# In-place masks without the row's constant in the forgetting heads' bias, and negated weights written by GpSimd

## The chip, the cores and the metric

The kernel runs on one core of one Trainium2 chip. The metric is device time in microseconds (us) of one execution. Before the change, three runs took 1092.12 us in the median (1089.89 to 1092.16). The engines are called as in the profile: PE is TensorE, DVE is VectorE, ACT is ScalarE, POOL is GpSimd; SP is SyncE, whose queue issues most of the DMAs.

## The reference

One decoder layer over 512 tokens of width 1024: a half-step SwiGLU FFN, then a mixer of two attention branches with gates, then a second half-step FFN. The change lies in the mixer. Its branch A is a forgetting attention with 8 heads of 64:

```python
def fox_attention(q, k, v, log_f):
    cum = jnp.cumsum(log_f, axis=1).transpose(0, 2, 1)
    ...
        logits = jnp.einsum('bqhd,bkhd->bhqk', q[:, start:end], k[:, :end]).astype(jnp.float32) * scale
        logits = logits + cum[:, :, start:end, None] - cum[:, :, None, :end]
        ...
        logits = jnp.where(kpos <= qpos, logits, NEG_INF)
        p = jax.nn.softmax(logits, axis=-1).astype(v.dtype)
        outs.append(jnp.einsum('bhqk,bkhd->bqhd', p, v[:, :end]))
```

For one query t, `cum[t]` is the same in all of its logits, and a softmax does not change when one number is added to a whole row. Branch B has 8 heads of sparse attention with a top-k indexer. The combined input projection `h @ w_in` feeds both.

## The kernel before

All matrix products take fp32 operands split in two parts, a rounded high part and the rest (wh and wl of a weight, xh and xl of the data). A product is three matmuls: wh by xh, wl by xh, wh by xl (`mm3`, whose three lines are inlined at L133 to L135 in the profile). PE's order is written out by hand; the other engines' orders (ACT, DVE, POOL, SP) come from a scheduler that goes by its own estimates of durations. Each engine and each queue works its instructions off in order, so an instruction that waits holds back all that stand behind it.

The stages in order: FFN 1 (to some 362 us), the mixer's projections and attention, the mixer's output, FFN 2 (from some 752 us).

**Weights.** `load_w` (L116) loads a chunk of 128 x 1024 from memory into a raw tile (ra, rb, rc in turn) by SP; ACT casts it to wh (L123). For most weights wl is raw minus wh by DVE or POOL (L128). For 16 chunks, those of the projections w_fk, w_fq, w_fv and w_dq (`by_dma`, set in `tm256`, L755), wl comes in two steps: ACT writes -wh (L125), and then a DMA issued by POOL reads the chunk from memory once more and adds it in flight (L126). The list `added` keeps these DMAs. A chunk is asked for two chunks before its products run (`weight`, L687); wh and wl have three buffers each.

**Heads.** `prod` runs projections in small steps of matmuls between the steps of the heads, so that PE has work while a softmax is under way. The loop over g (L1045) runs 16 heads, counted from 0: 0 to 7 are the forgetting heads, 8 to 15 the sparse ones. A head has four query blocks of 128 queries, done from the last (512 keys) to the first (128 keys): i = 3, 2, 1, 0, or by columns 512, 384, 256, 128. For each block, `softmax_block` (L907):

- takes the block's bias b from `bias(i)`,
- lets PE compute ps_qk (the logits' negative, L651 and L652),
- lets DVE write p = ps_qk + b and the row's least value mn in one instruction (L914); ACT then computes exp(mn - p) and the row's sum rs (L916), DVE its reciprocal (L917), POOL the product (L918, "normalisation").

The values of a head follow later, in `value_step`: PE transposes p (pt, L925), ACT and DVE split it (ph, L929; pl, L930), PE multiplies with the values (po, L935 and L936), and `head_out` copies the two halves of po (o, o3, L942 and L945), adds them (POOL, L946) and splits them (oAh, L949; oAl, L950). Every second head fetches new queries and keys (`get_q`, `get_k`): PE transposes them (ps_q, ps_k, L626), ACT and DVE split them (L645, L646: st, kh, kl). Their inputs kn were normed by `normed` (ACT squares sqh, L614; DVE sums ss, L616 and L617; POOL takes a power rh, L620, and scales kn, L724). In between DVE works off the indexer's top-k (L862, L864).

**The bias of a forgetting head.** `get_bias(g)` loads the head's row of cumulative sums from memory into all 128 partitions: the tile cb, 128 x 512, two buffers (L985). `bias(i)` writes a new tile b: POOL adds the negative of the block's own cumulative sums, `ncum`, one number for each query (L992), and then sets the part above the diagonal, the last 128 columns of the block, to 1e30 (L993). `ncum` is made once by DVE from `cum` (L849). The tiles b come from the pool "t" with six buffers, which other short-lived tiles share. So before the change cb is read by POOL only, and a buffer of cb is free as soon as POOL has made the four biases, which it often does far ahead of the blocks.

Of the kernel before, what the change touches and what calls it, by code (L numbers as in the profile page):

```python
# [11 lines left out]
F32 = mybir.dt.float32  # L12
F32R = mybir.dt.float32r
AF = mybir.ActivationFunctionType
OP = mybir.AluOpType
# [36 lines left out]
def tile_hybrid_layer(ctx: ExitStack, tc: tile.TileContext, a: dict):  # L52
# [14 lines left out]
    def tmp_tile(name):  # L67
        return tmp.tile([P, T], F32, tag="t", name=name)
# [47 lines left out]
    def load_w(src, n, m, raw=None, at=0, by_dma=False):  # L116
        f = n * m
        if raw is None:
            raw = raw_tile(next(raw_tags))
        wh, wl = (wpool.tile([P, W_COLS], F32R, tag=nm, name=nm)[:, at:at + 1024] for nm in ("wh", "wl"))  # L120
        with tc.high_priority(offset=1 if first else 30):
            nc.sync.dma_start(raw[:, :f].rearrange("p (n m) -> p n m", n=n), src)
            S.copy(wh[:, :f], raw[:, :f])  # L123
            if by_dma:
                S.mul(wl[:, :f], wh[:, :f].bitcast(F32), -1.0)  # L125
                added.append(G.dma_start(wl[:, :f].rearrange("p (n m) -> p n m", n=n), src, accum_op=OP.add))  # L126
            else:
                lo_eng[0].tensor_sub(wl[:, :f], raw[:, :f], wh[:, :f].bitcast(F32))  # L128
        return (wh[:, :f].rearrange("p (n m) -> p n m", n=n),
                wl[:, :f].rearrange("p (n m) -> p n m", n=n))  # L130
# [451 lines left out]
    with ExitStack() as merge_ctx, ExitStack() as mix_ctx, ExitStack() as att_ctx:  # L582
# [9 lines left out]
        dkl = at.tile([P, T], F32R, name="dkl")  # L592
        dvv = at.tile([P, NT, P], F32R, name="dvv")
        cum = at.tile([P, NT, H], F32, name="cum")
        ncum = at.tile([P, NT, H], F32, name="ncum")
        dram = att_ctx.enter_context(tc.tile_pool(name="dram", bufs=1, space=bass.MemoryType.DRAM))
        cum_rows = dram.tile([H, T], F32, name="cum_rows")
        wi = at.tile([P, NT, H], F32, name="wi")
# [4 lines left out]
        def mark(ins, late):  # L603

            marks.append((prod.total + late, ins))
# [217 lines left out]
        def forget():  # L823

            z = small.tile([P, NT, H], F32, tag="z", bufs=1, name="z")
            V.tensor_add(z, sg[:, :, 64:72], bf[:, None, :].to_broadcast([P, NT, H]))
            na = small.tile([P, NT, H], F32, tag="na", bufs=1, name="na")
            V.scalar_tensor_tensor(na, z, -1.0, z, op0=OP.mult, op1=OP.min)
            e = small.tile([P, NT, H], F32, tag="e", bufs=1, name="e")
            S.activation(e, na, AF.Exp)  # L830
            u1 = small.tile([P, NT, H], F32, tag="u1", bufs=1, name="u1")
            V.tensor_scalar(u1, e, 1.0, None, op0=OP.add)
            ln = small.tile([P, NT, H], F32, tag="ln", bufs=1, name="ln")
            S.activation(ln, u1, AF.Ln)
            cr = small.tile([P, NT, H], F32, tag="cr", bufs=1, name="cr")
            V.tensor_scalar(cr, u1, 1.0, None, op0=OP.subtract)
            V.tensor_sub(cr, e, cr)
            V.reciprocal(u1, u1)
            V.tensor_mul(cr, cr, u1)
            V.tensor_add(ln, ln, cr)  # L840
            lf = small.tile([P, NT, H], F32, tag="lf", bufs=1, name="lf")
            V.scalar_tensor_tensor(lf, z, 0.0, ln, op0=OP.min, op1=OP.subtract)
            yield
            pc = psum.tile([P, T], F32, tag="s", bufs=2, name="pc")
            for t in range(NT):
                for j in range(t + 1):
                    PE.matmul(pc[:, t * H:(t + 1) * H], trin if j == t else ones, lf[:, j], start=(j == 0), stop=(j == t))
            V.tensor_copy(cum, pc[:, :NT * H].rearrange("p (t h) -> p t h", t=NT))
            mark(V.tensor_scalar(ncum, cum, -1.0, None, op0=OP.mult), 0.5)  # L849
            yield  # L850
            ps = psum.tile([P, T], F32, tag="s", bufs=2, name="ps_ct")
            for t in range(NT):
                PE.transpose(ps[0:H, t * P:(t + 1) * P], cum[:, t], ident)
            cum_t = tmp_tile("cum_t")[0:H]
            S.copy(cum_t, ps[0:H])
            S.dma_start(cum_rows, cum_t)
# [126 lines left out]
        def get_bias(g):  # L983
            cb = at.tile([P, T], F32, tag="cb", bufs=2, name="cb")
            nc.sync.dma_start(cb, cum_rows[g:g + 1, :].to_broadcast([P, T]) if g < H else a["rel"][g - H])  # L985

            def bias(i):
                n = P * (i + 1)
                b = tmp_tile("b")
                if g < H:  # L990
                    with tc.issue_after(added[-2].ins) if g == 0 else nullcontext():
                        G.tensor_scalar(b[:, :n], cb[:, :n], 1.0, ncum[:, i, g:g + 1], op0=OP.mult, op1=OP.add)  # L992
                    G.affine_select(out=b[:, i * P:n], in_=b[:, i * P:n], compare_op=OP.is_ge, fill=BIG, base=0,  # L993
                                    pattern=[[-1, P]], channel_multiplier=1)
                else:
                    G.tensor_sub(b[:, :n], sc[i] if i else cpos, cb[:, T - n:T])
                return b[:, :n]
            return bias

# [192 lines left out]
```

## Time and profile before

| what | value |
|---|---|
| median of three runs | 1092.12 us (1089.89 to 1092.16) |
| the profiled execution | 1090.95 us, its span 1088.9 us |
| PE busy from 362 to 436 us (top-k scores, first projections) | 74.0 of 74 us |
| PE busy from 436 to 546 us (heads 0 to 7) | 101.7 of 110 us |
| PE busy from 660 to 752 us (gates, output) | 92.0 of 92 us |
| TensorE clock granted, mean of the span | 0.998 |

A row of the profile's groups reads: line, engine, operation, tiles written <- read with their shapes, count; then busy us and mean ns of one; then the idle time of the engine just before, and what ended it. A wait list names the waiting instruction, then the one that ended the wait: us in total, how often, the longest.

### The profile page before, as it was taken

The page shows a single profiled execution, that of the slowest core. Times are in us where ns is not written, and L with a number is a line of the kernel's source. Part 1 is how long each engine was busy: PE and PEld are TensorE (multiplying, and loading weights), DVE is VectorE, ACT ScalarE, POOL GpSimd, SP SyncE. Part 2 cuts the span into 40 slices and gives each one's busy share as a digit, 9 for nine tenths or more (in the row PEclk, how much of TensorE's full clock was granted, in tenths as well). Part 3 has the DMA queues.
Part 4 walks back from the last instruction along what each step waited for, and adds up shares of the span by engine and source line. Part 5 has one row for each costly group of instructions (what it writes and reads, how often), then busy time and mean ns, then how long its engine had stood idle before and what let it go on. Part 6 is the DMA issues. An engine that isn't in the chain of part 4 may idle for free.

```text
span 1088.9 us, 17859 instructions
## 1 busy us (share of the span) xinstructions
PE 1070.5 (98%) x6880; PEld 968.1 (89%) x6880; DVE 795.0 (73%) x1287; ACT 575.4 (53%) x908; POOL 209.4 (19%) x280
## 2 busy tenths in 40 slices
PE   9999999999999999999999999999999999999998
PEld 7889899989998899988778778889998899989997
DVE  6896478755967489879764765879986588865974
ACT  5554155522555675877655785455663155522650
POOL 0000000000001316677752740000110001000100
PEclk9999999999999999999999999999999999999999
DMA  7434335523442268765124211425574356633552
GB/s 239 118 98 134 108 88 147 139 95 97 125 108 90 99 134 195 173 143 133 49 59 135 87 60 48 135 89 153 138 166 137 90 135 160 165 97 98 145 126 78
DMA packets 43572, 131.01 MB, mean 120 GB/s; under 512 B 5336, under 2 KB 5720, under 8 KB 43488
## 3 DMA queue, kind: packets, MB, share of 16 engines
q1 hardware_dynamic: 35120, 107.58, 32.5%
q0 software_dynamic: 8208, 22.02, 11.7%
q8 instruction: 54, 0.88, 0.3%
q10 hardware_dynamic: 160, 0.28, 0.1%
q14 instruction: 30, 0.25, 0.1%
HBM read 117.79 MB, written 2.11 MB: 110 GB/s over the span
## 4 chain that ended last, share of the span: by engine, by line
PE 85%; DVE 6%; ACT 4%; issue 2%; DMA 2%; POOL 1%; SPq 0%; DVEq 0%; POOLq 0%; ACTq 0%
PE pd L133 7%; PE pd L135 7%; PE pd L134 7%; PE pB L133 5%; PE pB L134 5%; PE pB L135 5%; PE pC L133 3%; PE pA L133 3%; PE pA L134 3%; PE pC L134 3%; PE pC L135 3%; PE pA L135 3%; PE ps_f L133 3%; PE ps_f L134 3%; PE ps_f L135 3%
## 5 line engine op out<-in xcount | busy, mean ns | idle before, releaser
L133 PE MATMUL pd<-ah,wh 128*128 128x512 f32 (+1 forms) x294 | 113.2, 385 | 0.0
L134 PE MATMUL pd<-al,wh 128*128 128x512 f32 (+1 forms) x294 | 113.1, 385 | 0.0
L135 PE MATMUL pd<-ah,wl 128*128 128x512 f32 (+1 forms) x294 | 113.1, 385 | 0.0
L112 ACT CAST wh<-s 128x1024 fp32r<-128x1024 f32 x57 | 60.1, 1054 | 99.1 <-PE pB L134 51.3
L133 PE MATMUL pB<-tbh,wh 128*128 128x256 f32 x304 | 85.0, 280 | 0.6 <-DVE u L435 0.6
L134 PE MATMUL pB<-tbl,wh 128*128 128x256 f32 x304 | 84.8, 279 | 0.0
L135 PE MATMUL pB<-tbh,wl 128*128 128x256 f32 x304 | 84.7, 279 | 0.0
L133 PE MATMUL ps_t<-wh,xh 128*128 128x256 f32 (+1 forms) x288 | 81.7, 284 | 0.0
L134 PE MATMUL ps_t<-wl,xh 128*128 128x256 f32 (+1 forms) x288 | 81.0, 281 | 0.0
L135 PE MATMUL ps_t<-wh,xl 128*128 128x256 f32 (+1 forms) x288 | 81.0, 281 | 0.0
L271 POOL DMA_DIRECT2D al<-gu x26 | 22.2, 856 | 260.5 <-ACT al L270 248.9
L113 DVE TENSOR_TENSOR wl<-s,wh 128x1024 fp32r<-128x1024 f32 x57 | 69.4, 1218 | 1.7 <-ACT wh L112 1.5
L393 POOL DMA_DIRECT2D s<-in_w_pair_dram x11 | 9.6, 877 | 297.9 <-DVE wl L113 297.9
L135 PEld LDWEIGHTS pd<-ah,wl 128*128 128x128 f32 x294 | 55.2, 188 | 11.1
L134 PEld LDWEIGHTS pd<-al,wh 128*128 128x128 f32 x294 | 55.2, 188 | 10.8
L133 PEld LDWEIGHTS pd<-ah,wh 128*128 128x128 f32 x294 | 55.2, 188 | 10.8
L133 PEld LDWEIGHTS pB<-tbh,wh 128*128 128x128 f32 x304 | 57.1, 188 | 1.1 <-issue 0.9
L134 PEld LDWEIGHTS pB<-tbl,wh 128*128 128x128 f32 x304 | 57.2, 188 | 0.0
L135 PEld LDWEIGHTS pB<-tbh,wl 128*128 128x128 f32 x304 | 57.2, 188 | 0.0
L134 PEld LDWEIGHTS ps_t<-wl,xh 128*128 128x128 f32 x288 | 55.1, 191 | 0.5
L133 PEld LDWEIGHTS ps_t<-wh,xh 128*128 128x128 f32 x288 | 55.0, 191 | 0.5
L135 PEld LDWEIGHTS ps_t<-wh,xl 128*128 128x128 f32 x288 | 55.0, 191 | 0.0
(355 smaller groups left out, 3611.9 us busy)
## 6 DMA issues: line engine op xcount, KB each, us to landing
rc<-in_w_pair_dram SPq DMA_DIRECT2D x16, 512.0 KB, 3.6
rb<-in_w_pair_dram SPq DMA_DIRECT2D x16, 512.0 KB, 3.6
ra<-in_w_pair_dram SPq DMA_DIRECT2D x15, 512.0 KB, 3.6
rd<-in_w_pair_dram SPq DMA_DIRECT2D x15, 512.0 KB, 3.7
re<-in_w_pair_dram SPq DMA_DIRECT2D x14, 512.0 KB, 3.7
al<-gu POOLq DMA_DIRECT2D x26, 256.0 KB, 4.7
s<-in_w_pair_dram POOLq DMA_DIRECT2D x11, 512.0 KB, 5.6
ra<-in_w_down_dram SPq DMA_DIRECT2D x7, 512.0 KB, 3.6
```

Source lines behind the costliest of these rows:

```text
L112: S.copy(wh[:, :f], raw[:, :f])
L113: V.tensor_sub(wl[:, :f], raw[:, :f], wh[:, :f].bitcast(F32))
L133: PE.matmul(out, lh, rh, start=start, stop=False, **more)
L134: PE.matmul(out, lh, rl, start=False, stop=False, **more)
L135: PE.matmul(out, ll, rh, start=False, stop=stop, **more)
L271: G.dma_start(l, u, accum_op=OP.add)
L393: G.dma_start(t["s2"], load["b"][2], accum_op=OP.add)
```

## The change

For heads 0 to 7 the bias is no longer a tile of its own. `bias(i)` sets the 128 columns at the diagonal to 1e30 in cb itself and returns the first columns of cb; the number per query is left out, and with it `ncum` (a tile of the same size keeps its place). Since blocks run from the last to the first, the columns that one selection overwrites are not read by later blocks. But the block before has read them: the selection of block i - 1 writes columns that p of block i reads, so it waits for that p. And cb is now read by DVE, up to the last block of the head, before its buffer takes the row of the head after next. In `load_w` the negation -wh is made by POOL in place of ACT, with one multiplication by -1 and one by 1.

```diff
             if by_dma:
-                S.mul(wl[:, :f], wh[:, :f].bitcast(F32), -1.0)
+                G.tensor_scalar(wl[:, :f], wh[:, :f].bitcast(F32), -1.0, 1.0, op0=OP.mult, op1=OP.mult)
                 added.append(G.dma_start(wl[:, :f].rearrange("p (n m) -> p n m", n=n), src, accum_op=OP.add))
...
-        ncum = at.tile([P, NT, H], F32, name="ncum")
+        at.tile([P, NT, H], F32, name="pad")
...
-            V.tensor_copy(cum, pc[:, :NT * H].rearrange("p (t h) -> p t h", t=NT))
-            mark(V.tensor_scalar(ncum, cum, -1.0, None, op0=OP.mult), 0.5)
+            mark(V.tensor_copy(cum, pc[:, :NT * H].rearrange("p (t h) -> p t h", t=NT)), 0.5)
...
             def bias(i):
                 n = P * (i + 1)
-                b = tmp_tile("b")
                 if g < H:
                     with tc.issue_after(added[-2].ins) if g == 0 else nullcontext():
-                        G.tensor_scalar(b[:, :n], cb[:, :n], 1.0, ncum[:, i, g:g + 1], op0=OP.mult, op1=OP.add)
-                    G.affine_select(out=b[:, i * P:n], in_=b[:, i * P:n], compare_op=OP.is_ge, fill=BIG, base=0,
-                                    pattern=[[-1, P]], channel_multiplier=1)
-                else:
-                    G.tensor_sub(b[:, :n], sc[i] if i else cpos, cb[:, T - n:T])
+                        G.affine_select(out=cb[:, i * P:n], in_=cb[:, i * P:n], compare_op=OP.is_ge, fill=BIG, base=0,
+                                        pattern=[[-1, P]], channel_multiplier=1)
+                    return cb[:, :n]
+                b = tmp_tile("b")
+                G.tensor_sub(b[:, :n], sc[i] if i else cpos, cb[:, T - n:T])
                 return b[:, :n]
             return bias
```

PE's order stays the same. The lines after L849 move up by one, those after L992 by two. The scheduler lays out ACT, DVE, POOL and SP anew. Three places of that order follow; numbers behind a name tell one buffer's use from another's.

First, POOL ahead of the second half of the queries that heads 4 and 5 take (kn). Before, the rows behind head 2's biases:

```order
L126 DMA wl_4984<-in_w_dq_dram 128x1024
L993 AFFINE_SELECT b_5112<-b_5112 128x128
L620 TENSOR_TENSOR rh_4977<-ss_4974,nhalf_100 128x8
L126 DMA wl_5091<-in_w_dq_dram 128x1024
L724 TENSOR_TENSOR kn_4969<-kn_4969,rh_4977 128x512
```

And in the changed kernel, where cb_5120 is the row of head 4, cb_4901 that of head 3, and p_5044 the last block of head 2:

```order
L620 TENSOR_TENSOR rh_4956<-ss_4953,nhalf_100 128x8
L917 TENSOR_SCALAR p_5044<-p_5044,rs_4857 128x128
L125 TENSOR_SCALAR wl_5066<-wh_5065 128x1024
L990 AFFINE_SELECT cb_5120<-cb_5120 128x128
L990 AFFINE_SELECT cb_4901<-cb_4901 128x128
L724 TENSOR_TENSOR kn_4948<-kn_4948,rh_4956 128x512
```

A normalisation, a multiplication and two selections now stand between rh and kn. The first selection waits for the row of head 4, the second for p of head 3's first block.

Second, DVE around head 2's blocks of 256 and 128 columns. Before (head 2 is the one with rs_4874):

```order
L930 TENSOR_TENSOR pl_5010<-pt_5005,ph_5009 128x384
L950 TENSOR_TENSOR oAl_3405<-o_4933,oAh_3401 64x512
L616 TENSOR_REDUCE ss_4974<-sqh_4972 128x8
L930 TENSOR_TENSOR pl_5054<-pt_5050,ph_5053 128x256
L617 TENSOR_SCALAR ss_4974<-ss_4974 128x8
L864 MATCH_REPLACE sc2_3399<-m8_5016,sc2_3399 128x384
L862 MAX m8_5059<-sc3_3400 128x8
L914 ISA p_5026,mn_4873<-ps_qk_5023,b_5018 128x256
L914 ISA mn_4873 128x1
L914 ISA p_5069,mn_4873<-ps_qk_5066,b_5061 128x128
```

And in the changed kernel:

```order
L617 TENSOR_SCALAR ss_4942<-ss_4942 128x8
L913 ISA p_5003,mn_4856<-ps_qk_5000,cb_4685 128x256
L913 ISA mn_4856 128x1
L916 RECIPROCAL rs_4857<-rs_4857 128x1
L929 TENSOR_TENSOR pl_4989<-pt_4984,ph_4988 128x384
L949 TENSOR_TENSOR oAl_3405<-o_4914,oAh_3401 64x512
L616 TENSOR_REDUCE ss_4953<-sqh_4951 128x8
L913 ISA p_5044,mn_4856<-ps_qk_5041,cb_4685 128x128
```

The p of 256 columns moved from behind pl, oAl, ss and another pl to ahead of them, and the p of 128 columns to right behind ss.

Third, DVE around head 6's block of 256 columns. Before:

```order
L617 TENSOR_SCALAR ss_5854<-ss_5854 128x8
L128 TENSOR_TENSOR wl_5898<-ra_5896,wh_5897 128x1024
L930 TENSOR_TENSOR pl_5876<-pt_5871,ph_5875 128x384
L950 TENSOR_TENSOR oAl_3407<-o_5811,oAh_3403 64x512
L616 TENSOR_REDUCE ss_5865<-sqh_5863 128x8
L930 TENSOR_TENSOR pl_5915<-pt_5911,ph_5914 128x256
L617 TENSOR_SCALAR ss_5865<-ss_5865 128x8
L930 TENSOR_TENSOR pl_5944<-pt_5941,ph_5943 128x128
L914 ISA p_5890,mn_5760<-ps_qk_5887,b_5882 128x256
```

And in the changed kernel:

```order
L617 TENSOR_SCALAR ss_5801<-ss_5801 128x8
L913 ISA p_5835,mn_5711<-ps_qk_5832,cb_5553 128x256
L913 ISA mn_5711 128x1
L128 TENSOR_TENSOR wl_5843<-ra_5841,wh_5842 128x1024
L929 TENSOR_TENSOR pl_5823<-pt_5818,ph_5822 128x384
L949 TENSOR_TENSOR oAl_3407<-o_5760,oAh_3403 64x512
```

Here too the p stands ahead of the weight subtraction L128 and of the three pl that were in front of it.

## The prediction

> **What bounds the kernel now.** I read the busy times first, then the same times cut by stage, then what TensorE (PE) waits for in the one stage where it waits, and last the rows around each of those waits.
>
> ```profile
> PE 1070.5 (98%) x6880; PEld 968.1 (89%) x6880; DVE 795.0 (73%) x1287; ACT 575.4 (53%) x908; POOL 209.4 (19%) x280
> ```
>
> PE is busy for all but 18.4 us of the span. A change that touches no matrix product can win or lose only PE's idle time, so the question is where that idle time lies. The view by stretches has, for each stretch, its length and each engine's busy time (instructions):
>
> ```profile
> 362.00:436.00 74.00, 74.00 (x506) 68.97 (x505) 58.83 (x159) 51.76 (x97) 28.41 (x29) 0.98 0.61 150
> 436.00:546.00 110.00, 101.72 (x749) 94.33 (x748) 87.93 (x249) 83.17 (x177) 78.92 (x121) 1.00 0.52 125
> 546.00:660.00 114.00, 110.72 (x565) 90.72 (x564) 70.98 (x173) 75.89 (x156) 52.71 (x70) 1.00 0.26 82
> ```
>
> The changed lines run from 375 us to 546 us. Up to 436 us PE is never idle, so nothing can be won there. From 436 to 546 us, which are heads 0 to 7, it idles 8.3 us while DVE, ACT and POOL are busy for 80%, 76% and 72%. That is the whole stake. The 3.3 us after it lie in heads 8 to 15, and the rest at both ends of the span; their code stays. PE's waits in the stake (us in total, times, longest):
>
> ```profile
> PE pt L925 <- DVE st L646: 2.7, 3, 1.7
> PE ps_qk L651 <- DVE mn L914: 2.2, 2, 1.2
> PE po L936 <- DVE pl L930: 1.1, 2, 0.9
> PE ps_k L626 <- DVE pl L930: 0.8, 1, 0.8
> PE pt L925 <- DVE pl L930: 0.4, 1, 0.4
> PE ps_q L626 <- POOL kn L724: 0.4, 1, 0.4
> PE pt L925 <- POOL p L918: 0.3, 1, 0.3
> PE po L935 <- ACT ph L929: 0.2, 1, 0.2
> PE po L935 <- ACT o L945: 0.2, 1, 0.2
> ```
>
> Most end with DVE, but none with the biases (b) or with a weight. So the biases and the negated weights cost time only through the queue places they hold on POOL and ACT, ahead of what DVE needs. The six large waits one by one (start, duration, and in brackets the idle time before):
>
> ```profile
> 452.80 0.66 PE L626 MATMUL ps_k<-ident,kn 128*128 128x128 f32 x4 [0.81 <-DVE pl L930]
> 454.18 0.55 PE L925 MATMUL pt<-ident,p 128*128 128x128 f32 x3 [0.72 <-DVE st L646]
> 475.61 0.50 PE L651 MATMUL ps_qk<-kh,st 128*128 128x512 f32 x1 [1.25 <-DVE mn L914]
> 511.13 0.55 PE L925 MATMUL pt<-ident,p 128*128 128x128 f32 x3 [1.67 <-DVE st L646]
> 518.20 0.38 PE L936 MATMUL po<-pl,fv 128*128 128x256 f32 x1 [0.94 <-DVE pl L930]
> 530.51 0.50 PE L651 MATMUL ps_qk<-kh,st 128*128 128x512 f32 x1 [0.95 <-DVE mn L914]
> ```
>
> **What the change moves, in engine time.** The groups of instructions that it touches, and those nearest to the new one (busy us, mean ns):
>
> ```profile
> L125 ACT ACTIVATE wl<-wh 128x1024 fp32r<-128x1024 f32 x16 | 16.9, 1056 | 0.2
> L992 POOL TENSOR_SCALAR b<-cb,ncum 128x512 f32<-128x512 f32 (+3 forms) x32 | 19.4, 673 | 0.2
> L993 POOL TENSOR_SCALAR_AFFINE_SELECT b<-b 128x128 f32<-128x128 f32 x32 | 10.4, 378 | 0.3
> L918 POOL TENSOR_SCALAR p<-p,rs 128x512 f32<-128x512 f32 x16 | 11.6, 728 | 22.8 <-DVE rs L917 10.9 <-PE pt L925 10.3 <-PE po L936 1.6
> L918 POOL TENSOR_SCALAR p<-p,rs 128x128 f32<-128x128 f32 x16 | 6.5, 404 | 22.1 <-DVE rs L917 22.0
> L128 POOL TENSOR_TENSOR wl<-rc,wh 128x1024 fp32r<-128x1024 f32 x2 | 4.8, 2393 | 6.1 <-ACT wh L123 6.1
> ```
>
> ACT loses 16 negations, 16.9 us. POOL loses 32 bias additions, 19.4 us, and keeps the 32 selections. It gains 16 multiplications of 1024 columns, which the trace does not show. At least one costs the 0.73 us of half the columns (L918, 512), at most the 2.39 us of the two-input operation of that size (L128). I take the line through the two L918 rows, (728 - 404) / 384 = 0.84 ns a column, so 0.73 + 0.43 = 1.16 us, since L918 is the same operation; 16 make 18.6 us. POOL's total stays within 1 us, and what changes is what stands where. The Trainium skill, GPSIMD Engine Reference, section 3.1, gives 1.03 cycles a column for bodies of up to two operations; at that page's 1.2 GHz this is an estimated 0.88 us each and 14.1 us in all, 4.5 us less than by the rows. No run yet shows which holds for 1024 columns.
>
> **The weights** are costed at nothing. The multiplication starts when ACT's cast is done, as the negation did. The narrowest chunk is this one: its adding DMA on POOL, the landing of such DMAs (KB, us), and PE's first product with the chunk.
>
> ```profile
> 409.40 0.88 POOL L126 DMA_DIRECT2D wl<-in_w_fv_dram  x1 [2.83 <-DVE m L862]
> wl<-in_w_fv_dram POOLq DMA_DIRECT2D x4, 512.0 KB, 5.8
> 417.36 0.28 PE L133 MATMUL ps_t<-wh,xh 128*128 128x256 f32 x1
> ```
>
> Issued at 409.4 it lands at about 415.2 us, and PE begins at 417.4. So 2.2 us hide a later start; beyond that each 1 us late is 1 us of PE.
>
> **The ACT terms.** Rows of ACT around the first and the third wait, and of DVE behind them:
>
> ```profile
> 449.63 1.05 ACT L125 ACTIVATE wl<-wh 128x1024 fp32r<-128x1024 f32 x1
> 450.58 0.67 ACT L645 ACTIVATE st<-ps_q,gq 64x512 fp32r<-64x512 f32 x1
> 470.72 1.06 ACT L125 ACTIVATE wl<-wh 128x1024 fp32r<-128x1024 f32 x1
> 471.68 0.63 ACT L614 ACTIVATE sqh<-kn 128x512 f32<-128x512 f32 x1
> ```
>
> ```profile
> 472.34 0.69 DVE L616 TENSOR_REDUCE ss<-sqh 128x8 f32<-128x512 f32 x1 [0.77 <-ACT sqh L614]
> 475.15 0.40 DVE L914 CUSTOM_DVE_ANT_0 p<-ps_qk,b 128x256 f32<-128x256 f32 x1
> 516.59 1.22 DVE L128 TENSOR_TENSOR wl<-rc,wh 128x1024 fp32r<-128x1024 f32 x1
> ```
>
> At 449.63 the negation stands straight ahead of the query split that DVE sits waiting for. Without it the split and the pl behind it come 0.95 us earlier, and the wait of 0.81 us goes. The second wait grows by about 0.2 us, because another block's p now stands between the two splits on DVE: **-0.6 us** for the pair.
>
> PE had made the product of head 2's 256-column block here:
>
> ```profile
> 468.71 0.28 PE L652 MATMUL ps_qk<-kl,st 128*128 128x256 f32 x1
> ```
>
> Its p starts 6 us later, at 475.15, and PE waits for it at 475.61. In between p waited in DVE's queue behind rows that waited for sqh, itself behind the negation at 470.72. In the new order p stands ahead of pl, oAl and ss (second order excerpt). I take the 1.25 us as gone: **-1.25 us**. At 530.51 it is the same: p of head 6's 256 columns now stands ahead of the weight subtraction and of three pl (third excerpt): **-0.95 us**. At 518.20 the pl stood behind the subtraction of 516.59. The p ahead of it come earlier now, so it starts about 1 us earlier: **-0.9 us**. The two waits for ACT, 0.4 us in all, go with its 16.9 us, **-0.4 us**. The wait at 511.13 is for the second query split, which stays behind p and pl: **0**. Where PE waits 0.4 us for a pl (pt, L930), one more p comes ahead of it: **+0.5 us**. A remainder of 0.1 us elsewhere goes.
>
> **The POOL terms.** Three rows: POOL's scaling of the queries of heads 4 and 5, the landing of the broadcast row (KB, us), and the spread of one small DVE operation:
>
> ```profile
> 477.70 1.62 POOL L724 TENSOR_TENSOR kn<-kn,rh 128x512 f32<-128x512 f32 x1
> cb<-cum_rows SPq DMA_DIRECT2D x8, 256.0 KB, 3.7
> L617 DVE TENSOR_SCALAR ss<-ss x16: 142/160/850, 403.2 to 528.7; 128x8 f32<-128x8 f32 x12, 128x1 f32<-128x1 f32 x4
> ```
>
> The kn of 477.70 is what PE's ps_q wait of 0.4 us ended on. PE arrives there 1.9 us earlier by the terms above, but on POOL a multiplication (1.16 us) and two selections now stand ahead of kn (first excerpt), one of them waiting for a row that lands 3.7 us after the last p of head 2. I put kn's end at 478.5 us, 0.8 us earlier than now. So PE waits about 1.7 us there, and the 1.0 us of small waits around 480 us go: **+0.7 us**. With the multiplication at 0.73 us this becomes +0.3, at 2.39 us +1.9.
>
> The new wait in place: a selection writes what the p before it reads, so it waits for DVE, and p of the next block waits for it. Behind it on POOL wait the normalisations, kn, and the adding DMAs. Between two blocks lie 110 / 32 = 3.4 us, and a selection takes 0.38 us, so DVE does not feel it unless something long stands between. The one such place that I find is the normalisation of head 4's last block, which now stands behind head 6's first selection and its row: **+0.3 us**.
>
> The sum is -0.6 - 1.25 - 0.95 - 0.9 - 0.4 + 0.5 - 0.1 + 0.7 + 0.3 = **-2.7 us**. The profiled execution took 1090.95 us (span 1088.9, and 2.05 around it), so it would become 1088.25. The median of the three runs, 1092.12, lies 1.17 above it; I predict that median less 2.7, **1089.4 us**.
>
> **The rivals.**
>
> The waits only move (within 0.2%, which is 2.2 us and about what a measurement of this kernel can tell from no change). DVE is busy 80% of the stage, and wherever PE comes earlier it meets the next late row, as at kn. If half of the 3.1 us of the two p terms and the pl term come back that way, 1.1 us are left: 1091.0 us. The 87.93 us of DVE work, which the change leaves alone, speak for it.
>
> POOL's order becomes the bound (slower). The row of head g+2 can be loaded only after DVE's last p of head g; before, POOL was done with it early. Its first selection stands on POOL ahead of the second selection of head g+1, whose p comes two blocks, 6.9 us, later. From the issue, 3.7 us of landing and two selections of 0.38 take some 4.5 us. It decides from the point where another 2.4 us are lost between, which two multiplications ahead on POOL would be. If that costs 1 us at each of heads 2 to 7, the sum is +6 - 2.7 = +3.3 us: 1095.4 us. For it speaks POOL's long queue, against it that the slack holds at every place I followed.
>
> POOL's multiplications hold DVE up (slower). L617 takes 160 ns in the middle and 850 ns at worst, so some DVE rows are held by 0.7 us. Eight of the 16 negations lie in the stake; if each of the eight multiplications held a DVE row on the way to PE by 0.7 us, 5.6 - 2.7 = +2.9 us: 1095.0 us. Against it, the 19.4 us of additions that go could hold DVE in the same way. The Trainium skill, SBUF — State Buffer, section on the two separate sides, states that the pair of ports shared by VectorE and GpSimd is an exclusive lock, held for a whole instruction. The spread of L617 agrees with that; by it one long multiplication would hold a row longer than a short addition did.
>
> Everything that was late comes early. If also the wait at 511.13 and the new one at kn fall away, 2.7 + 1.7 + 1.7 = 6.1 us: 1086.0 us.
>
> **How the numbers follow.** The forecast, from 2.2 to 4.5 us faster, gets 0.37 and the larger gain 0.13: faster 0.50. Waits that only move get 0.35: same. POOL's order gets 0.10 and the ports 0.05: slower 0.15. For 8 in 10 I cut the largest gains at 1085.8 us and the slow cases at 1094.6 us, which also holds both ends of the multiplication's price (0.4 us to one side, 1.2 us to the other) and the 2.3 us by which the three runs differ.
>
> **What would show it.** Right: no L125 on ACT, PE's waits from 436 to 546 us at about 5.6 us instead of 8.3, none for mn, one of 1 to 2 us at ps_q for kn. Wrong: waits of PE or DVE ended by the selections, waits of PE for a weight (ps_t), or multiplications far from 1.16 us. If waits before p grow while the ones named here go, POOL's order is the cause.

## The result and the profile after

The changed kernel takes 1100.3 us in the median (four runs, 1097.86 to 1102.53), the kernel before, on the same chip, 1091.0 us (1089.04 to 1092.16). The ratio is 1.0089, 95% interval 1.0074 to 1.0104: 9 us slower, where 2.7 us faster were forecast, and above the range's upper end of 1094.6 us. The profiled execution took 1099.98 us (span 1098.2 us), 9.0 us more than the one before.

First the busy time of the engines on the page of the changed kernel, and then the same three stretches that the prediction shows:

```profile
PE 1073.6 (98%) x6880; PEld 971.1 (88%) x6880; DVE 797.2 (73%) x1286; ACT 561.4 (51%) x892; POOL 209.9 (19%) x264
```

```profile
362.00:436.00 74.00, 72.54 (x505) 67.36 (x504) 59.20 (x155) 43.08 (x87) 34.80 (x33) 1.00 0.62 147
436.00:546.00 110.00, 98.21 (x718) 92.61 (x717) 85.11 (x236) 74.27 (x161) 71.68 (x98) 0.95 0.52 123
546.00:660.00 114.00, 111.08 (x558) 91.40 (x557) 71.06 (x179) 73.21 (x155) 52.30 (x72) 0.99 0.28 84
```

The engines' work came out as expected: 14 us less on ACT, the same on POOL. The loss has three parts. From 436 to 546 us PE idles 11.8 us instead of 8.3, and ahead of that, where it never idled, 1.5 us: 5.0 us. PE's own busy time rises by 3.1 us for the same 6880 matmuls; the clock column, 0.95 instead of 1.00, says why. The third part is 1.0 us at the start of the span, where the code is the same, by the rows of the first 25 us before and after. Over all the traces of this study PE idles from 2.1 to 3.6 us there, so nothing shows that this part is the change's:

```profile
0.00:25.00 25.00, 22.44 (x91) 17.34 (x92) 16.49 (x23) 15.97 (x24) 1.65 (x12) 1.00 0.69 230
```

```profile
0.00:25.00 25.00, 21.41 (x87) 16.23 (x88) 16.48 (x23) 15.90 (x24) 1.66 (x12) 1.00 0.66 220
```

Together 9.1 of the 9.3 us by which the span grew. PE's waits from 436 to 546 us after the change:

```profile
PE po L935 <- DVE pl L929: 3.1, 3, 1.7
PE ps_k L626 <- DVE pl L929: 3.0, 2, 2.7
PE ps_q L626 <- POOL kn L724: 2.8, 1, 2.8
PE pt L924 <- DVE rs L916: 1.7, 2, 1.0
PE pt L924 <- DVE st L646: 0.9, 1, 0.9
PE pt L924 <- DVE pl L929: 0.2, 1, 0.2
```

None ends with mn any more, as forecast, but two of 2.7 and 2.8 us are new, and the longest of po for a pl is 1.7 us in place of 0.9. From the list of all waits from 362 to 560 us, those of POOL for a cast, and those of and for the selections:

```profile
POOL wl L125 <- ACT wh L123: 29.0, 11, 6.5
POOL cb L990 <- DMA cb<-cum_rows: 18.6, 8, 6.0
POOL cb L990 <- DVE mn L913: 6.7, 6, 1.6
DVE p L913 <- POOL cb L990: 6.5, 2, 4.1
```

POOL stands 18.6 us waiting for rows to land, and DVE's p waits twice for POOL. The longer of the two, in order of time, with SP's issue of head 2's row (cb), the selections and the p:

```profile
445.45 0.27 DVE L913 CUSTOM_DVE_ANT_0 p<-ps_qk,cb 128x128 f32<-128x128 f32 x1
...
445.75 0.33 SPq L984 DMA_DIRECT2D cb<-cum_rows  x1
...
447.05 0.69 DVE L913 CUSTOM_DVE_ANT_0 p<-ps_qk,cb 128x512 f32<-128x512 f32 x1 [0.39 <-PE ps_qk L652]
...
453.10 0.54 POOL L990 TENSOR_SCALAR_AFFINE_SELECT cb<-cb 128x128 f32<-128x128 f32 x2 [5.97 <-DMA cb<-cum_rows]
453.67 0.56 DVE L913 CUSTOM_DVE_ANT_0 p<-ps_qk,cb 128x384 f32<-128x384 f32 x1 [4.07 <-POOL cb L990]
...
455.88 1.09 PE L626 MATMUL ps_k<-ident,kn 128*128 128x128 f32 x4 [2.74 <-DVE pl L929]
```

The last p of head 0 at 445.45 frees the buffer, SP issues the row at once, and it lands 7.2 us later. POOL's row at 453.10 holds two selections: head 2's first, which needs that row, and right behind it in the queue head 1's second, which needed nothing but has waited all the same. So the p of head 1's second block starts 6.6 us behind that of the first, the next pl is late, and PE waits 2.74 us for it.

The second time it is head 5's row, issued behind the last p of head 3 and 6.6 us on its way. Its selection stands ahead of that for head 4's second block:

```profile
495.90 0.33 SPq L984 DMA_DIRECT2D cb<-cum_rows  x1
...
502.55 0.54 POOL L990 TENSOR_SCALAR_AFFINE_SELECT cb<-cb 128x128 f32<-128x128 f32 x2 [3.77 <-DMA cb<-cum_rows]
...
503.12 0.56 DVE L913 CUSTOM_DVE_ANT_0 p<-ps_qk,cb 128x384 f32<-128x384 f32 x1 [2.42 <-POOL cb L990]
...
505.33 0.50 PE L935 MATMUL po<-pl,fv 128*128 128x512 f32 x1 [1.69 <-DVE pl L929]
```

### The profile page after: what moved, and what is told of

Its sections match the earlier page's. It is cut to its first block, busy times and chain, and to the rows that moved or that the text cites. A ratio compares the mean times of both kernels' runs of the same rounds, so it can differ in the third digit from the quotient of the medians.

```text
span 1098.2 us, 17837 instructions
## 1 busy us (share of the span) xinstructions
PE 1073.6 (98%) x6880; PEld 971.1 (88%) x6880; DVE 797.2 (73%) x1286; ACT 561.4 (51%) x892; POOL 209.9 (19%) x264
## 4 chain that ended last, share of the span: by engine, by line
PE 84%; DVE 8%; ACT 2%; DMA 2%; issue 2%; POOL 1%; SPq 0%; DVEq 0%; POOLq 0%; ACTq 0%
PE pd L134 7%; PE pd L133 7%; PE pd L135 7%; PE pB L133 5%; PE pB L134 5%; PE pB L135 5%; PE pC L134 3%; PE pC L133 3%; PE pA L134 3%; PE pA L133 3%; PE pC L135 3%; PE pA L135 3%; PE ps_f L133 3%; PE ps_f L134 3%; PE ps_f L135 3%
```

## The experiments

Each time below is a median beside runs of the kernel before on the same chip, with the ratio to these and its 95% interval. The groups ran on different chips, so kernels of different groups are better compared by the ratio.

| kernel | us | ratio | interval |
|---|---|---|---|
| cb3 | 1102.17 | 1.0098 | 1.0077 to 1.0119 |
| mult_only | 1093.92 | 1.0026 | 1.0016 to 1.0035 |
| bias_only | 1090.62 | 1.0004 | 0.9993 to 1.0014 |
| cb3_act | 1090.42 | 1.0000 | 0.9990 to 1.0009 |
| in_turn | 1089.89 | 0.9997 | 0.9987 to 1.0006 |
| one_back | 1094.24 | 1.0044 | 1.0029 to 1.0060 |
| swap_act | 1093.57 | 1.0023 | 1.0013 to 1.0033 |
| in_turn_act | 1087.95 | 0.9972 | 0.9963 to 0.9981 |
| swap_free | 1089.89 | 0.9998 | 0.9988 to 1.0008 |
| in_turn_act3 | 1087.84 | 0.9975 | 0.9966 to 0.9984 |
| in_turn_act_ol | 1089.49 | 0.9990 | 0.9975 to 1.0005 |
| in_turn_cum | 1090.41 | 0.9998 | 0.9989 to 1.0007 |
| in_turn_first8 | 1090.72 | 0.9997 | 0.9987 to 1.0006 |
| in_turn_last8 | 1091.38 | 1.0007 | 0.9998 to 1.0016 |
| last8_stt | 1092.38 | 1.0015 | 1.0006 to 1.0023 |
| in_turn_stt | 1091.14 | 1.0000 | 0.9991 to 1.0009 |
| after_stt | 1099.54 | 1.0077 | 1.0055 to 1.0099 |
| in_turn_act_stt | 1088.81 | 0.9981 | 0.9972 to 0.9989 |

### First: which part of the change

Each part alone, and a third buffer for the rows. **mult_only** is the kernel before with the line of `load_w`; **bias_only** is the changed kernel without it:

```diff
-                S.mul(wl[:, :f], wh[:, :f].bitcast(F32), -1.0)
+                G.tensor_scalar(wl[:, :f], wh[:, :f].bitcast(F32), -1.0, 1.0, op0=OP.mult, op1=OP.mult)
```

> The kernel before with one line of the change alone: GpSimd writes the negated weights; the biases are as before, with ncum and tiles of their own. ROW and INPLACE: 1089 to 1092 us, as before or up to 2 us less, since ACT's negations go. MULT: 1096 to 1101 us, since POOL now works 16.9 us more than in the changed kernel's rivals and the biases of 19.4 us are still there (POOL busy about 227 us).

> The changed kernel with the negation back on ACT: the bias part of the change alone. ROW: the late rows stay, about 1097 to 1100 us. MULT: 1089 to 1092 us. INPLACE: about 1097 to 1100 us.

**cb3** (the changed kernel) and **cb3_act** (bias_only) give every third head a tile that is idle in this stage:

```diff
-            cb = at.tile([P, T], F32, tag="cb", bufs=2, name="cb")
+            cb = tmp.tile([P, T], F32, tag="ssq", bufs=1, name="cb") if g < H and g % 3 == 2 else at.tile([P, T], F32, tag="cb", bufs=2, name="cb")
```

> The changed kernel with a third buffer for the rows cb: heads 2 and 5 take a tile that is idle in this stage, so a row can be loaded one head earlier. ROW (a buffer of cb is held until DVE's last p of the head, so that the row of head g+2 comes late and holds up the selections and all that stands behind them on POOL): the waits of POOL for rows (18.6 us in the changed kernel) fall below 6 us, PE's waits in heads 0 to 7 fall from 13.2 to about 8 us, time about 1092 us, 8 us less than the changed kernel. MULT (GpSimd's multiplications fill POOL's queue ahead of kn and the normalisations): nothing changes, about 1100 us. INPLACE (each selection waits for the p of the block before): nothing changes, about 1100 us.

> The bias part of the change alone (negation on ACT) with the third buffer for cb. ROW: about 1091 us, the waits of POOL for rows gone, PE's waits in heads 0 to 7 at 7 to 9 us. MULT: about 1090 us whether or not the buffer is there, the same as the bias part alone. INPLACE: about 1098 us, the same as the bias part alone, and PE or DVE waits that selections end.

The bias part alone moves the time by nothing that can be told (ratio 1.0004), the multiplications alone cost 2.8 us by the ratio, and both together 9.7 us. So neither part alone is the cause, and INPLACE falls. MULT has the times of bias_only and cb3_act right, but mult_only is 2 us below its range, so it falls as the whole story. ROW has only the time of cb3_act right (1090.42 us), and not by its reason: POOL still waits 15.8 us for rows there, and bias_only takes as long without the buffer. In cb3 the third buffer took nothing away. But it did not do what was meant. With a buffer more, the scheduler moved the first selections one head earlier in POOL's queue, so that they again stand just behind the issue of their rows:

```profile
440.13 0.29 POOL L990 TENSOR_SCALAR_AFFINE_SELECT cb<-cb 128x128 f32<-128x128 f32 x1 [6.27 <-DMA cb<-cum_rows]
```

This is head 2's first selection in cb3: its row is issued at 431.69 us and lands 8.4 us later, and head 0's later selections stand behind it. POOL's waits for rows grew to 24.3 us. The buffer was the wrong knob; the place in the queue had to be held.

What differs between bias_only and the changed kernel at the place shown above is one order. In bias_only head 1's second selection stands ahead of head 2's first one:

```profile
442.78 0.33 SPq L984 DMA_DIRECT2D cb<-cum_rows  x1
...
444.47 0.69 DVE L913 CUSTOM_DVE_ANT_0 p<-ps_qk,cb 128x512 f32<-128x512 f32 x1
...
445.25 0.29 POOL L990 TENSOR_SCALAR_AFFINE_SELECT cb<-cb 128x128 f32<-128x128 f32 x1 [0.38 <-DVE mn L913]
...
448.26 0.56 DVE L913 CUSTOM_DVE_ANT_0 p<-ps_qk,cb 128x384 f32<-128x384 f32 x1 [1.23 <-PE ps_qk L652]
...
449.66 0.29 POOL L990 TENSOR_SCALAR_AFFINE_SELECT cb<-cb 128x128 f32<-128x128 f32 x1 [4.12 <-DMA cb<-cum_rows]
```

The row takes 6.8 us to land here too, and POOL waits 4.1 us for it, but p (448.26) waits for PE alone. In all, POOL waits for rows longer in this kernel (20.1 us) than in the changed one, and it costs nothing.

### Second: the order of the selections

**in_turn** (the changed kernel) and **in_turn_act** (bias_only) hold each head's first selection on POOL behind the last one of the head before:

```diff
-                    with tc.issue_after(added[-2].ins) if g == 0 else nullcontext():
-                        G.affine_select(
+                    with tc.issue_after(added[-2].ins if g == 0 else sel[g - 1, 0].ins) if i == NT - 1 else nullcontext():
+                        sel[g, i] = G.affine_select(
```

> The changed kernel, with each head's first selection held on POOL behind the last selection of the head before it. ORDER (a first selection that waits for a row stands on POOL ahead of the next block's selection, and so the landing of the row, up to 7.2 us, falls on DVE's p): no p waits for a selection by more than 1 us, p of head 1's second block starts within 3.5 us of the first one (6.6 us in the changed kernel), the 2.7 us wait of PE for ps_k goes; what is left is the multiplications' own cost as in the kernel with them alone: about 1094 us. MULT-SUM (the multiplications cost 9 us in any kernel whose selections wait for p, whatever the order of the selections): 1098 to 1101 us.

> The bias part of the change alone (negation on ACT), with each head's first selection held behind the last selection of the head before it: the likely best. ORDER: the few waits of p for selections go: 1088 to 1090.5 us. MULT-SUM: 1090 to 1092 us, no change to the bias part alone.

**one_back** does it at one place, for head 2's first selection (`sel[1, 2]` for g = 2 alone). **swap_act** does the reverse: in bias_only it makes head 2's first selection when its row is asked for, and holds head 1's second selection behind it:

```diff
+            if g == 2:
+                bias(NT - 1)
...
-                    with tc.issue_after(added[-2].ins) if g == 0 else nullcontext():
+                    with tc.issue_after(added[-2].ins if g == 0 else sel[2, 3].ins) if g == 0 or (g, i) == (1, 2) else nullcontext():
```

> The changed kernel with one order alone turned back: head 2's first selection stands on POOL behind head 1's second selection, as it does with the negation on ACT. ORDER: PE's 2.7 and 0.9 us waits at 456 to 458 us and the low clock behind them go: 1094 to 1097 us, 3 to 6 less than the changed kernel's 1100. MULT-SUM: 1099 to 1101 us.

> The bias part of the change alone (negation on ACT), with one order forced: head 2's first selection stands on POOL ahead of head 1's second selection, as the scheduler has it in the changed kernel. ORDER: p of head 1's second block waits for the row of head 2, some 3 to 5 us, and PE 2 to 4 us: 1093 to 1096 us, against 1090.6 without. MULT-SUM: no change, 1090 to 1092 us.

All four went as ORDER expects, and in_turn further: 1089.9 us where 1094 was expected. In in_turn seven selections stand at other places on POOL than in the changed kernel; every other order, on all engines, is the same. One order turned back wins 5 us by the ratio, 6 by the medians; all of them win the whole 10. In one_back PE's 2.7 us wait is gone, but its wait of 0.9 us for st stays, and head 2's row now holds up later blocks: PE waits 2.27 us for a pl at 462.53 us, with the low clock behind it. One order forced costs 2 us by the ratio (1.0023 against 1.0004), 3 by the medians, with the same rows as in the changed kernel, the p at 451.53 waiting 4.0 us and PE 2.66 us:

```profile
450.96 0.54 POOL L992 TENSOR_SCALAR_AFFINE_SELECT cb<-cb 128x128 f32<-128x128 f32 x2 [5.60 <-DMA cb<-cum_rows]
451.53 0.56 DVE L913 CUSTOM_DVE_ANT_0 p<-ps_qk,cb 128x384 f32<-128x384 f32 x1 [4.01 <-POOL cb L992]
...
453.74 0.63 PE L626 MATMUL ps_k<-ident,kn 128*128 128x128 f32 x4 [2.66 <-DVE pl L929]
```

in_turn_act beats both kernels: 1087.95 us, ratio 0.9972. It is the one kernel of these four with neither the harmful order nor the multiplications.

### Third: the row or the place

**swap_free** keeps the forced order of swap_act, but gives head 2's row a tile of its own, so that it is loaded at the start; heads 2 to 4 are held at their places on POOL, and the place of head 1's second selection stays (the first selections of heads 3 and 4 and one kn still moved by a few places):

```diff
+            cb = tmp.tile([P, T], F32, tag="ssq", bufs=1, name="cb") if g == 2 else at.tile([P, T], F32, tag="cb", bufs=2, name="cb")
```

> The kernel with the forced order (negation on ACT, head 2's first selection ahead of head 1's second on POOL), but with a tile of its own for head 2's row, so that the row is loaded at the start and not after DVE's last p of head 0. ROW (what costs is that the selection waits for the row's release and landing): p of head 1's second block starts within 4 us of the first one, PE's 2.7 us wait at 453 us and the low clock behind it go, 1089.5 to 1091.5 us. PLACE (a selection at that place costs by itself, through POOL's time or its wait for a p): 1093 to 1094 us, as with the forced order.

**in_turn_act3** is in_turn_act with the third buffer of cb3; the orders of POOL and DVE are the same as without it.

> Selections in turn, negation on ACT, and a third buffer for the rows; the orders of POOL and DVE are the same as without it. ROW: once the selections are in turn, a row has a whole head to land, so that loading it another head earlier brings nothing: 1087 to 1089 us, the same as with two buffers. If the release of the two buffers still cost something: 1 us less or more.

Both went as ROW expects. With the row there in time, the same order costs nothing: 1089.89 us, and the p of head 1's second block starts 3.8 us behind the first (444.49 to 448.29) instead of 6.6 in swap_act. And with the selections in turn, an earlier row brings nothing (1087.84 against 1087.95). So it takes both, the late row and the place in the queue. A last kernel of this group, **in_turn_act_ol**, moves the subtraction for oAl from DVE to POOL:

```diff
-            (V if gg < H else G).tensor_sub(o2[1][h // 2][own], o[own], o2[0][h // 2][own].bitcast(F32))
+            (V if gg < 0 else G).tensor_sub(o2[1][h // 2][own], o[own], o2[0][h // 2][own].bitcast(F32))
```

> Selections in turn, negation on ACT, and the subtraction that makes oAl (L949) moved from DVE to POOL for heads 0 to 7, into the time that the bias additions left free there. If DVE's queue is what PE waits for now: PE's waits for DVE rows fall by 1 to 2 us, 1085.5 to 1087.5 us. If POOL's queue carries it on (the subtraction stands ahead of normalisations or kn): 1088 to 1091 us.

It is no gain, 1089.49 us: PE's wait for kn grew from 1.2 to 2.1 us, so the subtraction went into POOL's queue ahead of kn.

### Fourth: what the multiplications cost

They cost 2.8 us in mult_only and 1.9 us in in_turn against in_turn_act, with no wait of PE for a weight (ps_t) in any trace. What PE waits for in mult_only, most of all:

```profile
PE ps_qk L651 <- DVE mn L914: 5.7, 4, 1.9
PE pt L925 <- DVE st L646: 1.9, 3, 0.9
PE ps_ct L853 <- DVE cum L848: 1.5, 1, 1.5
```

So with the biases left as they were, PE waits 5.7 us for mn, where it waited 2.2 before. One order on DVE differs with them: the copy of cum stands behind the subtraction dkl, and PE waits 1.5 us for cum at 426 us, in the changed kernel, cb3, mult_only and in_turn. **in_turn_cum** puts dkl behind cum:

```diff
-            evac_split(transposed(lambda t: sd[0][:, t].rearrange("p a d -> p (a d)"), "ps_dk"), hg[:, 3:4], dkh, dkl)
+            ps = transposed(lambda t: sd[0][:, t].rearrange("p a d -> p (a d)"), "ps_dk")
+            S.mul(dkh, ps, hg[:, 3:4])
+            yield
+            with tc.issue_after(copied[0].ins):
+                mark(V.scalar_tensor_tensor(dkl, ps, hg[:, 3:4], dkh.bitcast(F32), op0=OP.mult, op1=OP.subtract), 1.0)
```

> Selections in turn and GpSimd's multiplications, with one order on DVE turned back: the copy of cum stands ahead of the subtraction dkl (0.73 us), as it does with the negation on ACT. QUEUE (the multiplications cost their 2 us not by their own length but by the order that the scheduler makes around them, and 1.5 us of it is PE's wait for cum at 426 us): that wait falls to 0.8 us or less, time 1088.5 to 1089.5 us against 1089.9. LENGTH (the multiplications cost by the 16.9 us that they hold POOL): the wait may fall, the time stays at 1089.9 us, and kn or the normalisations are what PE waits for.

The wait went, the time stayed (1090.41 us): QUEUE missed its time. This does not show that the wait was free. PE idles 2.3 us less in this trace than in in_turn's, but it is busy 2.8 us longer with the same matmuls, since the granted clock was 0.50 in two stretches of 3.41 us, from 421.87 and from 561.81 us; in in_turn there is no such stretch between the two ends of the span. one_back suggests that the two trade: it has dkl ahead of cum as in the changed kernel, a stretch at 0.50 from 421.88 us, and no wait for cum. **in_turn_first8** and **in_turn_last8** give GpSimd eight chunks and ACT the other eight:

```diff
-                G.tensor_scalar(wl[:, :f], wh[:, :f].bitcast(F32), -1.0, 1.0, op0=OP.mult, op1=OP.mult)
+                G.tensor_scalar(wl[:, :f], wh[:, :f].bitcast(F32), -1.0, 1.0, op0=OP.mult, op1=OP.mult) if len(added) < 8 else S.mul(wl[:, :f], wh[:, :f].bitcast(F32), -1.0)
```

(`>= 8` for the last eight.)

> Selections in turn; GpSimd negates the first eight chunks only (up to about 436 us), ACT the last eight. AHEAD (the multiplications cost ahead of the heads, at PE's wait for cum and by what starts late there): 1089.5 to 1090.5 us, as with all sixteen on GpSimd, and the 1.5 us wait is there. HEADS (they cost in the heads, by POOL's queue in front of kn and the normalisations): 1087.5 to 1088.5 us, as with none.

> Selections in turn; ACT negates the first eight chunks, GpSimd the last eight (in heads 0 to 7). AHEAD: 1087.5 to 1088.5 us, as with none on GpSimd. HEADS: 1089.5 to 1090.5 us, and PE's waits from 436 to 546 us by 1 to 2 us above those with none.

Neither half is free: 1090.72 and 1091.38 us, each as much as all sixteen. A cost by length would have halved, so AHEAD and HEADS both fall as the single answer. The clock blurs this too: the trace of in_turn_first8 has three stretches of 3.41 us at 0.50, none of them in the heads, in_turn_act's has one. The trace of in_turn_last8 shows for its half a stall that has nothing to do with the multiplications' own rows. L617, a DVE operation on 128 x 8, takes 2.09 us:

```profile
452.17 2.09 DVE L617 TENSOR_SCALAR ss<-ss 128x8 f32<-128x8 f32 x1
452.34 1.34 POOL L724 TENSOR_TENSOR kn<-kn,rh 128x512 f32<-128x512 f32 x1
...
453.37 0.86 POOL L917 TENSOR_SCALAR p<-p,rs 128x384 f32<-128x384 f32 x1
454.29 0.76 DVE L646 SCALAR_TENSOR_TENSOR st<-ps_q,gq,st 64x512 fp32r<-64x512 f32 x1
...
455.10 0.55 PE L924 MATMUL pt<-ident,p 128*128 128x128 f32 x3 [2.79 <-DVE st L646]
```

It ends at 454.26 us, 0.03 us behind the normalisation of 453.37, st starts only then, and PE waits 2.79 us for st. That POOL holds it is read from these times, not shown by a run. In the changed kernel such a hold stands ahead of the second new wait, that for kn at 485.42 us: L617 takes 1.75 us, until 479.56, the power rh follows on POOL, then a normalisation, a multiplication, two selections that wait for head 4's row, and kn:

```profile
477.81 1.75 DVE L617 TENSOR_SCALAR ss<-ss 128x8 f32<-128x8 f32 x1
...
479.64 1.80 POOL L620 TENSOR_TENSOR rh<-ss,nhalf 128x8 f32<-128x8 f32 x1
...
481.66 1.15 POOL L125 TENSOR_SCALAR wl<-wh 128x1024 fp32r<-128x1024 f32 x1
...
483.82 0.54 POOL L990 TENSOR_SCALAR_AFFINE_SELECT cb<-cb 128x128 f32<-128x128 f32 x2 [1.01 <-DMA cb<-cum_rows]
484.33 1.04 POOL L724 TENSOR_TENSOR kn<-kn,rh 128x512 f32<-128x512 f32 x1
```

To test the hold, L617 was made another form of instruction, with a small tile of the constant; apart from that tile's one filling, the engines' orders stay. It is done to in_turn_last8 (**last8_stt**), in_turn (**in_turn_stt**), the changed kernel (**after_stt**) and in_turn_act (**in_turn_act_stt**):

```diff
-            ins = V.tensor_scalar(ss[:, :nh], ss[:, :nh], 1.0 / DH, EPS, op0=OP.mult, op1=OP.add)
+            ins = V.scalar_tensor_tensor(ss[:, :nh], ss[:, :nh], 1.0 / DH, eps[:, 0, :nh], op0=OP.mult, op1=OP.add)
```

> Selections in turn, GpSimd negates the last eight chunks, and L617 (ss / 64 + eps on DVE) is a scalar_tensor_tensor with a small tile of eps in place of a tensor_scalar. HOLD (POOL holds L617, and that is what the last eight cost): L617 takes 0.1 to 0.4 us everywhere, the 2.8 us wait of PE for st at 455 us and the low clock behind it go, 1088 to 1089.5 us against 1091.4. NOT (the holds are hidden, or the other form is held too): 1090.5 to 1092 us.

> Selections in turn, all sixteen multiplications on GpSimd, and L617 in the other form. HOLD: 1088 to 1089.3 us against 1089.9, PE's waits from 436 to 546 us 1 us less. NOT: 1089.5 to 1090.5 us.

> The changed kernel with L617 in the other form, nothing else. HOLD: the late kn at 485 us comes 1 to 1.5 us earlier, PE's wait there falls from 2.8 to about 1.5 us and the clock does not drop behind it: 1096 to 1098 us against 1100; the rest, from the order of the selections, stays. NOT: 1099 to 1101 us.

> Selections in turn, negation on ACT, and L617 in the other form; in this kernel L617 was held by 0.4 us at most. HOLD and NOT alike: 1087 to 1088.5 us, no change; if it falls below 1087, other holds that the trace hides were on the path too.

No time fell clear of the noise (after_stt's six runs spread from 1092.50 to 1101.95 us). But the new form is held just as long, 2.07 us at worst in last8_stt, 1.98 in in_turn_stt and 1.74 in after_stt, so nothing was taken away, and the four runs say nothing on what the holds cost. It stays open.

## Why the prediction was wrong

**What bounds the kernel** was read rightly for a gain. "That is the whole stake" was too small for a loss: 8.3 us limit what idle time can be won there, but a loss is not limited by what is idle now. Only 3.5 us of it are idle time of that stage. 1.5 us came ahead of it, where "nothing can be won", and 3.1 us came as a lower clock. So the sentence that such a change "can win or lose only PE's idle time" did not hold.

**The p terms** (-1.25 and -0.95 us) were right at their place: no PE wait ends with mn any more, in the changed kernel nor in bias_only. But bias_only is no faster, and PE idles there about as long as before: 0.3 us of difference from 436 to 546 us. The waits moved to kn (1.5 us), to normalised p (1.2 us) and to rs (1.6 us). The pl term (-0.9 us) failed at its place: that matmul still waits 1.03 us for its pl in the changed kernel, at 525.86 us. The wait of 1.67 us for the second query split, which was to stay, is gone. So of the bias part the rival "the waits only move" was the true account.

**The POOL terms** hold the step that failed: all waits of DVE's p for a selection were put at +0.3 us, because "DVE does not feel it unless something long stands between" and only one such place was found. In the changed kernel p waits 4.07 and 2.42 us for selections that stand behind a row, at two other places, and PE 2.7 and 1.7 us behind them. The rival "POOL's order becomes the bound" described the mechanism that the runs then showed (swap_act, swap_free, in_turn): the row loaded only after DVE's last p, its selection ahead of the next block's, the p behind it. It got 0.10 because "the slack holds at every place I followed", and that was worked out with 3.7 us of landing, the median of before, when the rows were issued long ahead of their use. The rival named its own point of decision, 2.4 us more. At the place that mattered the landing was 7.2 us, 3.5 more, and the condition was met; that place, between heads 0 and 2, was not among the excerpts followed. The room was too large as well: 6.9 us were put in for two blocks, but in the changed kernel DVE stands waiting for that p from 449.60 us, 4.2 us behind the last p of head 0, and in swap_free, where no selection holds it, it starts 5.8 us behind. The rival's price was also wrong: 1 us at each of six heads was put in, and it came as 2.7 us at one place (0.8 before), 1.7 us at a second (none before), and 1.0 of the 2.8 us at kn. The 0.9 us wait for st behind the first is not part of it: it was 0.7 before, and one_back has it too.

**The price of kn** (+0.7) was put at 478.5 us for its end, and it ended at 485.4. The multiplication ahead of it takes 1.06 us in the mean, close to the 1.16 assumed:

```profile
L125 POOL TENSOR_SCALAR wl<-wh 128x1024 fp32r<-128x1024 f32 x16 | 16.9, 1055 | 29.0 <-ACT wh L123 29.0
```

The Trainium skill's 0.88 us (GPSIMD Engine Reference, section 3.1), an estimate from that page, is lower than the row. By 485 us everything was later, PE too; what counts is how long PE waits for kn, 2.8 us where 1.7 were forecast. The two rows below show the same wait in one_back, which has no stall at the first place, and in in_turn, where no selection ahead of kn waits for a row:

```profile
482.79 0.44 PE L626 MATMUL ps_q<-ident,kn 128*128 128x128 f32 x2 [2.75 <-POOL kn L724]
```

```profile
479.13 0.44 PE L626 MATMUL ps_q<-ident,kn 128*128 128x128 f32 x2 [1.74 <-POOL kn L724]
```

So the first stall is not what made PE wait here. In in_turn the wait is the 1.7 us that were forecast. The 1.0 us more goes with head 4's row: it landed in 6.2 us where 3.7 were put in, and its selection, ahead of kn, waited 1.0 us for it. So the landing was too short here too.

**A term was missing**: the clock, 3.1 us of the 9. The last section tells of it.

**The ACT terms** (-0.6 and -0.4 us) and the weights "at nothing" belong to the multiplications. PE's two waits for ACT did go, but the whole was forecast as a relief and is none: mult_only is 0.26% slower (0.16 to 0.35). No weight was late, so the part on their cover stands; the cost lies in waits for mn and cum there, and no run settles which order makes them. The port rival (0.05) is half seen: L617 takes up to 1.75 us after the change, 0.85 before, but while POOL works on kn and the normalisations, not on a multiplication. What that adds up to is not settled.

## What to carry to other kernels

When a change keeps a buffer in use until a later reader, look for the instruction that waits for its next filling, and ask what stands behind it in its queue: a wait that is harmless in one place of an in-order queue cost 2 to 6 us one place further up here (swap_act, one_back). Price the transfer with its worst landing under load, not with the median of a trace in which it was early. And where a scheduler lays out the queues, tie such an instruction by hand to the place where its buffer is free in time: the same masks in the same two buffers cost 10 us or nothing.

## What was not expected of the hardware

**A PE wait of some 2 us can cost more than it lasts.** The stretches around the 2.74 us wait, cut where the granted clock changes (the column before the last two):

```profile
451.68:455.09 3.41, 1.46 (x13) 1.26 (x11) 1.35 (x4) 0.92 (x4) 1.99 (x3) 1.00 0.44 162
455.09:458.50 3.41, 1.75 (x8) 1.38 (x8) 3.35 (x8) 1.32 (x2) 3.41 (x6) 0.50 0.00 0
458.50:461.92 3.42, 3.42 (x16) 3.23 (x15) 3.28 (x10) 1.77 (x4) 3.42 (x5) 0.50 0.75 127
461.92:465.33 3.41, 3.41 (x30) 3.41 (x29) 1.59 (x8) 1.92 (x4) 2.20 (x3) 1.00 0.80 189
```

In the first stretch of 3.41 us PE is idle for 1.95 us; in the next two it runs at half the clock, 16 matmuls where the last has 30. Away from both ends of the span, the halved stretches of every trace are 3.41 or 6.83 us long and lie on a fixed grid of 3.41 us. In heads 0 to 7, over all the traces of this study, a cell of that grid with 1.95 us or more of PE idle time was followed by one at half clock, 13 times out of 13, and at full clock none with 1.76 us or less was. It depends on the grid: in last8_stt a PE wait of 2.77 us falls across two cells, and the clock stays. The limit is not the same everywhere: behind the heads, at 557 to 570 us, cells with 1.57 to 1.59 us of idle time were followed by a halving in nine traces, the changed kernel's among them. A cell at half clock loses up to 1.7 us, half its length. In the changed kernel three such cells lie in heads 0 to 7, in the kernel before none, and in_turn, with none either, has PE busy for 1068.2 us where the changed kernel has 1073.6. The Trainium skill, TensorE: Matmul & The Clock Gate, part 1, gives a free-running window of 3.41 us and says that the clock halves after an idle window, with idle gaps to be kept under about 3.4 us. The length agrees with the traces; the gap does not: 1.95 us of idle time in a window was enough. Not every halving has such a cause: in seven traces, that of the kernel before among them, there is one near 422 us, where the records show PE busy throughout.

**Landings.** A row of 256 KB of the forgetting heads took from 3.0 to 8.4 us from issue to landing in these runs. The stretch from issue to landing for head 2's row in the changed kernel, and for one of the quickest, in cb3 (the last two columns are the busy share of the DMA engines and GB/s):

```profile
445.75:452.95 7.20, 7.20 (x61) 7.10 (x60) 3.46 (x11) 5.24 (x12) 1.25 (x3) 1.00 0.80 181
```

```profile
510.99:513.99 3.00, 3.00 (x26) 2.91 (x25) 2.69 (x7) 1.77 (x5) 0.00 (x0) 1.00 0.27 92
```

The slow one shares the DMA engines with a chunk's adding DMA and two weight loads, the quick one hardly with anything. This is a reading of the traces; no run took the other transfers away.

**Holds.** L617, 0.16 us in the middle, took up to 2.09 us, over the time of several POOL instructions and not only one. The Trainium skill, SBUF — State Buffer, section on the two separate sides, has the loser of the shared ports wait for one whole instruction of the other; no POOL instruction in the rows above is longer than 1.8 us, and in the row at 452.17 none longer than 1.34 us ran beside it. If POOL is what holds it, one instruction is not enough.
